# RG-LRU gate products as four 64x64 quadrants instead of block-diagonal 128x128 weights

## The chip, the cores and the metric

The kernel runs on one core of a Trainium2 chip. The metric is the time of one execution on the device in microseconds (us). Three runs of the kernel before are given, with their median.

## What is computed

The reference is a trunk of two layers of width 1024 on 512 latent and 256 context tokens (768 tokens in all). Each layer normalizes and modulates its input, projects it into three groups of heads (latent attention, a bidirectional mLSTM, a bidirectional RG-LRU), joins their outputs in one projection, and ends with an MLP. The change is in the RG-LRU. Its 256 channels form four blocks of 64, and each gate multiplies each block by its own 64x64 weights:

```python
LRU_BLOCKS, LRU_BD = 4, 64
...
def gates(xs, d):
    r = jax.nn.sigmoid(block_diag(xs, w_a[d], b_a[d]))
    i = jax.nn.sigmoid(block_diag(xs, w_x[d], b_x[d]))
```

`xs` is the branch's input after a convolution over four tokens; `d` is one of two directions. From `r` come the decay of a linear recurrence over the tokens (a = exp(-8 r softplus(-lam))) and the factor sqrt(1 - a^2); the recurrence runs over a and sqrt(1 - a^2) times i times xs, once forward and once backward, and the two results are added.

## The kernel before, in words

Channels lie on the 128 partitions and tokens on the columns, context first. The program is written as parts (Python generators) that yield an estimate of the time of what they have just emitted. `weave` takes a step of whichever part is behind, so parts are emitted side by side; a tile framework then sets the order on each engine and the semaphores. Engines are PE (TensorE), DVE (VectorE), ACT (ScalarE), POOL (GpSimd) and SP (SyncE, which issues most DMAs).

The stage of a layer that matters here (line 1172) weaves these parts:

- `in_kvq` makes keys and values of the mLSTM: products `kvp` (L178) of 128 tokens by 256 channels, in three passes over split weights (`whi`, `wlo`) and split inputs (`uh`, `ul`). For each of two halves there are six blocks of tokens with 24 matmuls each. ACT copies the results out (`kt` at L503, `vt` at L505). The weights are loaded by SP (L155), cast by ACT (`whi`, L158), and DVE takes the difference (`wlo`, L159).
- `ml_gates` (from L656) computes the mLSTM's gates. POOL's DMAs fetch `ig` and `fg` (L667); ACT takes three functions (L670 to L672); DVE makes `lf` (L674) and scans over `m` (L682, L684) and `bb` (L687, L688), then `st` and `bb` (L695, L697), the sum `lf` (L705); ACT takes exponentials into `st` (L706 for the first table `st1`, L717 for the second, `st2`, whose argument `ig` DVE makes in L710 to L716). PE transposes both tables into `colp` (L726), DVE copies that out (`colt`, L728), and PE makes `woldp` (L741).
- `lru` (L563) is the RG-LRU.
- In layer 0 only, a filler `mod_vec` makes modulation vectors: SP loads `modw` (512 KB a step, L247), PE multiplies (`modp`, L249, four matmuls on four groups of 32 columns); at the end of a vector DVE copies `modst` (L254) and PE transposes it (`modt`, L257).

In `lru` the convolution of a chunk of 128 channels (two blocks of 64) runs on DVE (L596, L599) into `xs`. For each direction and each gate (r, then i) PE makes one psum tile `lrup` (L608): a matmul on the 256 context columns and one on the 512 latent columns, whose 128x128 weights hold two 64x64 blocks on the diagonal and zeros elsewhere. There are 2 layers x 2 chunks x 2 directions x 2 gates = 16 such products. ACT turns each into `sig` with a Tanh (L613). Then ACT takes an exponential `lru_a` (L622) and a Tanh (L623), DVE multiplies (L624, L628, L629), ACT takes square roots (L633, L635), DVE multiplies (L640) and scans (L642, L645), and L649 adds the two directions.

The tiles `lru_a` and `lru_w` share a pool of three buffers (tag `aw`); the `lrup` tiles and the others of two banks share three psum buffers (tag `p2`). The weights `lruw` of a layer are one DMA of 512 KB (L565).

Of the kernel before, what the change touches and what calls it, by code (L numbers as in the profile page):

```python
# [9 lines left out]
F32 = mybir.dt.float32  # L10
F32R = mybir.dt.float32r
I32 = mybir.dt.int32
AF = mybir.ActivationFunctionType
# [4 lines left out]
L = 2  # L18
# [9 lines left out]
# how fast parts of the program go beside others, by layer  # L28
# [32 lines left out]
def trunk_kernel(ctx, tc, ins, out, dbg=None):  # L61
# [42 lines left out]
    # x^T, chunks of 128 channels, tokens [context | latent]  # L104
# [9 lines left out]
    # adds up rows r, 32 + r, 64 + r, 96 + r  # L114
# [6 lines left out]
    # ------------------------------------------------------------------ interleaving  # L121
    # A part of the program is a generator that yields about how long (us) what it emitted takes.
# [16 lines left out]
    def weave(*gens):  # L139
        """emit parts side by side, at equal pace; a filler only as long as the others last."""  # L140
# [10 lines left out]
    # ---------------------------------------------------------- small helpers  # L151
    def split_raw(src, shape):
        """(hi, lo) of weights from DRAM: hi has the bits that one pass of a product carries."""
# [8 lines left out]
    def split_act(src, a, b, tag, name, shape=None, tag2=None, after=None):  # L162
        """(hi, lo) of src, into columns a:b of new tiles: hi by ScalarE, lo by VectorE."""
# [11 lines left out]
    def mm3(dst, w, r, first, last):  # L175
        """dst += w.T @ r from the (hi, lo) parts of both."""
        for i, (a, b) in enumerate(PASSES):
            mm(dst, w[a], r[b], start=first and i == 0, stop=last and i == 2)  # L178

    def dense(ps, wk, rk, segs, M=128, po=PO):  # L180
        """ps[:M, po + t] = sum_k wk[k].T @ rk[k][:, t]; wk, rk: lists of (hi, lo)."""
# [8 lines left out]
    def rsqrt(v, n):  # L190
        """v ** -0.5 for n columns."""
# [4 lines left out]
    class Norm:  # L196
        """(mean of squares over channels + eps) ** -0.5 of each token, on every partition."""
# [17 lines left out]
        def columns(self, seg, out=None):  # L215
            """by tokens on partitions, a column per block of 128."""
# [9 lines left out]
        def spread(self, seg, ps, y):  # L226
            """on every partition, tokens along the columns."""
# [7 lines left out]
    # ------------------------------------------------------------- modulation  # L235
# [6 lines left out]
    def mod_vec(l, v, pace):  # L242
        """one of the six modulation vectors of a layer, a step per 128 rows of its weights."""
# [24 lines left out]
    def mod_rows(rows):  # L268
        """silu of both conditions along the columns, on every partition."""
# [10 lines left out]
    def mod_dot(l, v, pace, rows):  # L280
        """one of the six modulation vectors of a layer, a step per 128 of its channels."""
# [18 lines left out]
    def mod_load(j, tags):  # L300
        """the weights of 256 channels of the first two modulation vectors of the first layer."""
# [994 lines left out]
```

## Time and profile before

| | us |
|---|---|
| runs of the kernel | 1642.92, 1652.01, 1648.88 |
| median | 1648.88 |
| span of the profiled execution, from its first to its last recorded instruction | 1647.5 |
| PE busy in it | 1600.6 (97%) |
| DVE busy | 1075.7 (65%) |
| ACT busy | 583.2 (35%) |
| POOL busy | 63.6 (4%) |

The page gives no other time of the profiled execution than its span, so the span stands for it here; the median of the runs is 1.4 us above it. The trace gives each instruction's start and duration, grouped where the same instruction follows itself, and for idle time the engine and line that ended it. Several records belong to one matmul where its operands are f32 (a matmul of the gate products leaves two).

### The profile page before, as it was taken

The page shows a single profiled execution, that of the slowest core. Times are in us where ns is not written, and L with a number is a line of the kernel's source. Part 1 is how long each engine was busy: PE and PEld are TensorE (multiplying, and loading weights), DVE is VectorE, ACT ScalarE, POOL GpSimd, SP SyncE. Part 2 cuts the span into 40 slices and gives each one's busy share as a digit, 9 for nine tenths or more (in the row PEclk, how much of TensorE's full clock was granted, in tenths as well). Part 3 has the DMA queues.
Part 4 walks back from the last instruction along what each step waited for, and adds up shares of the span by engine and source line. Part 5 has one row for each costly group of instructions (what it writes and reads, how often), then busy time and mean ns, then how long its engine had stood idle before and what let it go on. Part 6 is the DMA issues. An engine that isn't in the chain of part 4 may idle for free.

```text
span 1647.5 us, 23128 instructions
## 1 busy us (share of the span) xinstructions
PE 1600.6 (97%) x9202; PEld 1335.2 (81%) x9202; DVE 1075.7 (65%) x2122; ACT 583.2 (35%) x878; POOL 63.6 (4%) x106
## 2 busy tenths in 40 slices
PE   8998999999999999999999998999999999999997
PEld 4666897788788888888888886887788888888887
DVE  4784577766797676666666478966877644444446
ACT  4462224444442212222122146622645432323223
POOL 1201010000000000000000001101000000000000
PEclk9999999999999999999999999999999999999998
DMA  9447111101344343333333131322102323222222
GB/s 314 129 158 231 64 58 47 50 14 63 105 146 149 116 141 115 109 122 118 134 120 128 65 116 40 89 70 77 65 14 90 116 90 102 90 94 99 90 103 102
DMA packets 58587, 170.48 MB, mean 103 GB/s; under 512 B 6720, under 2 KB 19776, under 8 KB 58480
## 3 DMA queue, kind: packets, MB, share of 16 engines
q1 hardware_dynamic: 55216, 161.26, 28.6%
q0 software_dynamic: 2112, 6.70, 1.4%
q8 instruction: 72, 1.18, 0.3%
q10 hardware_dynamic: 1152, 1.05, 0.2%
q14 instruction: 35, 0.29, 0.1%
HBM read 165.44 MB, written 2.15 MB: 102 GB/s over the span
## 4 chain that ended last, share of the span: by engine, by line
PE 81%; issue 2%; DVE 2%; ACT 1%; DMA 1%; POOL 0%; POOLq 0%; DVEq 0%; ACTq 0%
PE ff L186 51%; PE inp L186 6%; PE outp L186 6%; PE first L440 3%; PE py L178 2%; PE S L998 2%; PE kvp L178 2%; PE pT L1020 1%; PE S L1002 1%; PE pn L841 1%; PE S L1000 1%; PE qrp L186 1%; DMA modjunk<-in_crow 1%; PE sT L818 1%; PE lrup L608 1%
## 5 line engine op out<-in xcount | busy, mean ns | idle before, releaser
L158 ACT CAST whi<-raw 128x1024 fp32r<-128x1024 f32 x191 | 200.6, 1051 | 721.6 <-PE ff L186 578.6
L159 DVE TENSOR_TENSOR wlo<-raw,whi 128x1024 fp32r<-128x1024 f32 x191 | 233.1, 1221 | 158.4 <-ACT whi L158 153.9
L186 PE MATMUL ff<-hh,whi 128*128 128x512 f32 (+1 forms) x800 | 242.2, 348 | 0.0
L186 PE MATMUL ff<-hl,whi 128*128 128x512 f32 (+1 forms) x800 | 242.0, 348 | 0.0
L186 PE MATMUL ff<-hh,wlo 128*128 128x512 f32 (+1 forms) x800 | 242.0, 348 | 0.0
L289 DVE SCALAR_TENSOR_TENSOR modjunk<-modw,cb 128x512 f32<-128x512 f32 x224 | 154.7, 690 | 106.3 <-DMA modw<-in_w_modT 101.3
L186 PE MATMUL ff<-uh,whi 128*128 128x512 f32 (+1 forms) x696 | 210.9, 357 | 1.0 <-ACT hrelu L1077 1.0
L186 PE MATMUL ff<-uh,wlo 128*128 128x512 f32 (+1 forms) x696 | 210.2, 356 | 0.0
L186 PE MATMUL ff<-ul,whi 128*128 128x512 f32 (+1 forms) x696 | 209.4, 355 | 0.0
L408 DVE SCALAR_TENSOR_TENSOR x<-ff,mod,x 128x256 f32<-128x256 f32 (+1 forms) x200 | 123.1, 639 | 103.1 <-PE ff L186 103.0
L186 PEld LDWEIGHTS ff<-hl,whi 128*128 128x128 f32 x800 | 150.4, 188 | 20.8
L186 PEld LDWEIGHTS ff<-hh,wlo 128*128 128x128 f32 x800 | 150.3, 188 | 20.6
L186 PEld LDWEIGHTS ff<-hh,whi 128*128 128x128 f32 x800 | 150.3, 188 | 20.5
L186 PEld LDWEIGHTS ff<-uh,whi 128*128 128x128 f32 x696 | 130.8, 188 | 21.8 <-ACT hrelu L1077 1.7
L186 PEld LDWEIGHTS ff<-uh,wlo 128*128 128x128 f32 x696 | 131.0, 188 | 20.6 <-DVE wlo L159 0.5
L186 PEld LDWEIGHTS ff<-ul,whi 128*128 128x128 f32 x696 | 130.7, 188 | 20.5
L186 PE MATMUL inp<-uh,whi 128*128 128x256 f32 (+1 forms) x224 | 71.6, 376 | 3.7 <-ACT whi L158 3.7
L186 PE MATMUL inp<-ul,whi 128*128 128x256 f32 (+1 forms) x224 | 69.1, 366 | 0.0
L186 PE MATMUL inp<-uh,wlo 128*128 128x256 f32 (+1 forms) x224 | 68.8, 364 | 0.3 <-DVE wlo L159 0.3
L193 POOL TENSOR_TENSOR rsq<-rsv,nhalf 128x2 f32<-128x2 f32 (+2 forms) x16 | 14.2, 886 | 1310.1 <-DVE rsv L223 1308.6
L178 PE MATMUL kvp<-whi,uh 128*128 128x256 f32 x192 | 60.0, 313 | 4.2 <-ACT sig L613 2.9
L440 PE MATMUL first<-uh,wlo 128*128 128x256 f32 (+3 forms) x192 | 61.9, 325 | 0.6 <-DVE wlo L159 0.6
(316 smaller groups left out, 2767.2 us busy)
## 6 DMA issues: line engine op xcount, KB each, us to landing
raw<-in_w_ff2c SPq DMA_DIRECT2D x72, 512.0 KB, 3.5
raw<-in_w_ff1c SPq DMA_DIRECT2D x64, 512.0 KB, 3.5
modw<-in_w_modT SPq DMA_DIRECT2D x56, 512.0 KB, 3.7
modw<-in_w_mod SPq DMA_DIRECT2D x24, 512.0 KB, 4.4
raw<-in_w_outc SPq DMA_DIRECT2D x24, 512.0 KB, 3.5
raw<-in_w_inc SPq DMA_DIRECT2D x21, 512.0 KB, 3.5
modw<-in_w_mod SPq DMA_DIRECT2D x32, 256.0 KB, 5.1
raw<-in_w_inkv SPq DMA_DIRECT2D x8, 512.0 KB, 3.5
```

What stands on the lines that cost most here:

```text
L158: nc.scalar.copy(hi, raw)
L159: V.tensor_tensor(lo, raw, hi.bitcast(F32), op=OP.subtract)
L178: mm(dst, w[a], r[b], start=first and i == 0, stop=last and i == 2)
L186: mm(ps[:M, po + t0:po + t1], wk[k][a], rk[k][b][:, t0:t1], start=(k == 0 and i == 0), stop=(k == n - 1 and i == 2))
L289: V.scalar_tensor_tensor(junk, w[:, 512 * i:512 * i + 512], 1.0, rows[2 * r + i], op0=OP.mult, op1=OP.mult, accum_out=acc[:, m, i, r:r + 1])
L408: V.scalar_tensor_tensor(x[m][:, s[0]:s[1]], ps[:, po + s[0]:po + s[1]], modv[l][:, v, m, r:r + 1], x[m][:, s[0]:s[1]], op0=OP.mult, op1=O ...
L440: mm(ps[:M, PO + s[0]:PO + s[1]], wk[k][a][:, :M], self.rk[k][b][:, s[0]:s[1]], start=(k == 0 and i == 0), stop=(k == NK - 1 and i == 2))
L608: mm(ps[:, PO + a:PO + b], wl[:, g, d, c], xs[:, a:b], start=True, stop=True)
L818: mm(sT[h][:, PO + 128 * b:PO + 128 * b + 128], kT[p][hp, bs], z["q"][p][hp, bs], start=True, stop=True)
L841: mm(w["pn"][:, 65 * b:65 * b + 65], wT[:, 128 * b:128 * b + 128], z["vt"][p][:, b, j], start=True, stop=True)
L998: mm(S[:, PO + a:PO + e], z["qk"][h][wa][:, qs], ckv[ra][:, a:e], start=(i == 0), stop=False)
L1000: mm(S[:, PO + a:PO + e], z["qr"][h][:, qs], kr[0][:, a:e], start=False, stop=False)
```

## The change

The block-diagonal weights go. TensorE's array is used as four quadrants of 64x64: the upper or lower half of the partitions feeds it, the left or right half of the columns comes out. The weights `lruw` hold gate r's blocks on partitions 0 to 63 and gate i's on 64 to 127, half of the bytes of before (256 KB a layer). Row half g therefore always computes gate g, and it needs both blocks of channels on its own 64 partitions. Block o on partitions 64 o is there in `xs` for g = o; for the other two quadrants two DMAs on POOL's queue copy `xs` into a tile `xsw` with its halves exchanged (64 partitions x 768 x 4 bytes = 192 KB each). `xsw` takes one of the three `aw` buffers. Per direction both gates' psum tiles are made together by eight matmuls of 64x64, and two Tanh follow. The steps yield 0.65 instead of 1.3, so the weaving of the other parts around them moves too.

```diff
@@ def lru(l, z, t0):
-        wl = wp.tile([128, 2, 2, 2, 128], F32, tag="raw", bufs=3, name="lruw")
+        wl = wp.tile([128, 2, 2, 128], F32, tag="raw", bufs=3, name="lruw")
...
+            sw = slot("aw", "xsw")
+            for g in range(2):
+                gdma(sw[64 * g:64 * g + 64], xs[64 - 64 * g:128 - 64 * g])
             sg, sp_ = {}, {}
             for d in range(2):
+                pss = [ps2("lrup") for _ in range(2)]
+                for a, b in BOTH:
+                    for g in range(2):
+                        for o in range(2):
+                            rows, outs = slice(64 * g, 64 * g + 64), slice(64 * o, 64 * o + 64)
+                            mm(pss[g][outs, PO + a:PO + b], wl[rows, d, c, outs], (xs if g == o else sw)[rows, a:b],
+                               start=True, stop=True)
                 for g in range(2):
-                    ps = ps2("lrup")
-                    for a, b in BOTH:
-                        mm(ps[:, PO + a:PO + b], wl[:, g, d, c], xs[:, a:b], start=True, stop=True)
                     st = slot("ls", "sig", shape=[SB // 4])
...
-                    act(s, ps[:, PO:], AF.Tanh, scale=0.5, bias=hb[:, 4 * g + 2 * d + c:4 * g + 2 * d + c + 1])
+                    act(s, pss[g][:, PO:], AF.Tanh, scale=0.5, bias=hb[:, 4 * g + 2 * d + c:4 * g + 2 * d + c + 1])
                     sg[d, g] = s
-                    yield 1.3
+                    yield 0.65
...
@@ layout of the weights on the host
-    wl = np.zeros((L, 128, 2, 2, 2, 128), f)
+    wl = np.zeros((L, 128, 2, 2, 128), f)
...
-                wl[:, o:o + 64, gi, d, b // 2, o:o + 64] = i[nm][:, d, b]
+                wl[:, 64 * gi:64 * gi + 64, d, b // 2, o:o + 64] = i[nm][:, d, b]
```

Dependencies in the changed program: the copies wait for the last step of the chunk's convolution on DVE; the second chunk's `xsw` takes the buffer of the first chunk's `lru_w`, so it waits for DVE's product `sig<-sig,lru_w` (L640 of before); the psum tiles of the second direction wait for the Tanh of the first.

The order on the engines changes in the two stages with keys and values alone. On PE in layer 0, where the first chunk's gates are made, before:

```order
L608 MATMUL lrup_705<-xs_672,lruw_630 128x256
L178 MATMUL kvp_712<-whi_604,uh_168 128x256
L178 MATMUL kvp_712<-wlo_605,uh_168 128x256
L178 MATMUL kvp_712<-whi_604,ul_169 128x256
L178 MATMUL kvp_712<-whi_604,uh_170 128x256
L178 MATMUL kvp_712<-wlo_605,uh_170 128x256
L178 MATMUL kvp_712<-whi_604,ul_171 128x256
L608 MATMUL lrup_719<-xs_672,lruw_630 128x256
L249 MATMUL modp_663<-modw_692,cs_92 32x256 x4
L608 MATMUL lrup_705<-xs_672,lruw_630 128x512
L608 MATMUL lrup_719<-xs_672,lruw_630 128x512
```

And with the change:

```order
L615 MATMUL lrup_708<-xs_672,lruw_630 64x256
L249 MATMUL modp_663<-modw_692,cs_92 32x256 x4
L249 MATMUL modp_663<-modw_751,cs_92 32x256 x4
L615 MATMUL lrup_708<-xsw_705,lruw_630 64x256
L615 MATMUL lrup_708<-xs_672,lruw_630 64x512
L615 MATMUL lrup_708<-xsw_705,lruw_630 64x512
L249 MATMUL modp_663<-modw_787,cs_92 32x256
L615 MATMUL lrup_709<-xsw_705,lruw_630 64x256
L615 MATMUL lrup_709<-xs_672,lruw_630 64x256
L615 MATMUL lrup_709<-xsw_705,lruw_630 64x512
L615 MATMUL lrup_709<-xs_672,lruw_630 64x512
```

The key/value products that stood between the gate matmuls now come behind all eight of the first direction; only products for the modulation stand among them.

On DVE in layer 1, from the chain of the mLSTM's gates to the sum `lf` (`sig` and `gb` belong to the RG-LRU), before:

```order
L599 SCALAR_TENSOR_TENSOR xs_9100<-xp_8502,cols_74,xs_9100 128x256
L682 SCALAR_TENSOR_TENSOR m_8860<-lf_8765,ig_8766 4x768
L684 SCALAR_TENSOR_TENSOR m_8860<-lf_8765,ig_8766 4x256
L687 SCALAR_TENSOR_TENSOR bb_8862<-fg_8768,lf_8765 4x768
L684 SCALAR_TENSOR_TENSOR m_8860<-lf_8765,m_8860,ig_8766 4x512
L688 SCALAR_TENSOR_TENSOR bb_8862<-fg_8768,lf_8765 4x768
L624 SCALAR_TENSOR_TENSOR sig_8876<-sig_8876,xs_8821 128x768
L695 TENSOR_TENSOR st1_8920<-ig_8766,bb_8862 36x768
L628 TENSOR_TENSOR gb_8819<-lru_a_8933 128x768
L697 TENSOR_TENSOR bb_8862<-bb_8862,m_8860 36x768
L629 SCALAR_TENSOR_TENSOR gb_8819<-gb_8819,sig_8857 128x768
L705 TENSOR_TENSOR lf_8765<-st1_8920,bb_8862 4x768 x2
```

And with the change, where the next row is the sum `lf` (L714 there):

```order
L159 TENSOR_TENSOR wlo_9126<-raw_9123,whi_9125 128x1024
L691 SCALAR_TENSOR_TENSOR m_8892<-lf_8787,ig_8788 4x768
L693 SCALAR_TENSOR_TENSOR m_8892<-lf_8787,ig_8788 4x256
L633 SCALAR_TENSOR_TENSOR sig_8905<-sig_8905,xs_8843 128x768
L693 SCALAR_TENSOR_TENSOR m_8892<-lf_8787,m_8892,ig_8788 4x512
L696 SCALAR_TENSOR_TENSOR bb_8894<-fg_8790,lf_8787 4x768
L697 SCALAR_TENSOR_TENSOR bb_8894<-fg_8790,lf_8787 4x768
L637 TENSOR_TENSOR gb_8841<-lru_a_8939 128x768
L704 TENSOR_TENSOR st1_8959<-ig_8788,bb_8894 36x768
L638 SCALAR_TENSOR_TENSOR gb_8841<-gb_8841,sig_8889 128x768
L706 TENSOR_TENSOR bb_8894<-bb_8894,m_8892 36x768
L633 SCALAR_TENSOR_TENSOR sig_8928<-sig_8928,xs_8843 128x768
```

A difference of weights (`wlo`) has come in ahead of the scans, and a second product `sig` ahead of `lf`; the piece of the convolution has gone ahead of the rows shown.

On ACT in layer 1, from the exponential of `st1` on, before:

```order
L706 ACTIVATE st1_8920<-lf_8765 36x768
L717 ACTIVATE st2_8921<-ig_8766 36x768
L503 COPY kt_8740<-kvp_8982 128x128
L503 COPY kt_8741<-kvp_8982 128x128
L158 CAST whi_9088<-raw_9086 128x1024
L633 ACT_TABLE_LOAD
L633 ACTIVATE lru_w_9000<-lru_w_9000 128x768
L635 ACTIVATE gb_8819<-gb_8819 128x768
```

And with the change:

```order
L715 ACTIVATE st1_8959<-lf_8787 36x768
L503 COPY kt_8762<-kvp_9020 128x128
L503 COPY kt_8763<-kvp_9020 128x128
L642 ACT_TABLE_LOAD
L642 ACTIVATE lru_w_8988<-lru_w_8988 128x768
L726 ACT_TABLE_LOAD
L726 ACTIVATE st2_8960<-ig_8788 36x768
L644 ACT_TABLE_LOAD
L644 ACTIVATE gb_8841<-gb_8841 128x768
```

The square root of `lru_w` now stands between the two exponentials, with a table load ahead of it and one behind it.

## Rows read from the trace of the kernel before

**Rows 1.** The page: busy time of each engine, its share of the span, instructions.

```profile
PE 1600.6 (97%) x9202; PEld 1335.2 (81%) x9202; DVE 1075.7 (65%) x2122; ACT 583.2 (35%) x878; POOL 63.6 (4%) x106
```

**Rows 2.** Chain of waits, layer 1: start us, us, what.

```profile
1022.03 2.56 PE lrup L608 x4
...
1025.92 1.29 PE lrup L608 x4
1027.21 5.19 PE kvp L178 x44
1032.40 1.65 issue
```

**Rows 3.** Timeline of PE, layer 0: start, us, instruction, [idle before, releaser].

```profile
102.31 0.44 PE L257 MATMUL modt<-ident,modst 128*128 128x128 f32 x2 [3.93 <-DVE modst L254]
...
113.47 0.39 PE L178 MATMUL kvp<-whi,uh 128*128 128x256 f32 x1
...
140.28 0.88 PE L186 MATMUL inp<-uh,whi 128*128 128x256 f32 x2 [2.24 <-ACT whi L158]
```

**Rows 4.** Timeline of PE, layer 1.

```profile
1020.57 0.39 PE L178 MATMUL kvp<-whi,uh 128*128 128x256 f32 x1 [2.90 <-ACT sig L613]
...
1034.05 0.70 PE L726 MATMUL colp<-ident,st 100*128 100x100 f32 x6 [1.65 <-issue]
...
1036.13 0.71 PE L726 MATMUL colp<-ident,st 100*128 100x100 f32 x6 [0.17 <-issue]
```

**Rows 5.** Timeline of PE, layer 0, ahead of the first gate product.

```profile
71.67 0.28 PE L178 MATMUL kvp<-wlo,uh 128*128 128x256 f32 x1
71.88 0.64 PE L249 MATMUL modp<-modw,cs 128*32 128x256 f32 x8
...
72.67 0.28 PE L178 MATMUL kvp<-whi,uh 128*128 128x256 f32 x1
```

**Rows 6.** DMA issues from 66 to 100 us: transfer, count, KB, us to landing.

```profile
fg<-kg POOLq DMA_DIRECT2D x2, 12.0 KB, 3.2
```

**Rows 7.** DMA issues from 1060 to 1080 us.

```profile
sig<-kg POOLq DMA_DIRECT2D x2, 192.0 KB, 4.3
```

**Rows 8.** DMA issues from 120 to 140 us.

```profile
sig<-kg POOLq DMA_DIRECT2D x2, 192.0 KB, 10.0
```

**Rows 9.** Stretches: length, busy PE, PEld, DVE, ACT, POOL, granted clock, DMA share, GB/s.

```profile
73.00:80.00 7.00, 6.77 (x46) 4.27 (x45) 5.92 (x11) 6.68 (x9) 1.27 (x4) 1.00 0.73 198
...
130.00:140.00 10.00, 6.64 (x57) 5.07 (x56) 5.19 (x23) 2.95 (x5) 0.06 (x1) 1.00 0.96 286
...
1020.00:1025.00 5.00, 4.43 (x16) 3.22 (x17) 4.91 (x4) 3.96 (x7) 0.28 (x3) 0.66 0.01 3
```

**Rows 10.** Timeline of DVE, layer 0.

```profile
73.24 0.75 DVE L599 SCALAR_TENSOR_TENSOR xs<-xp,cols,xs 128x512 f32<-128x512 f32 x1
...
81.30 1.75 DVE L687 TENSOR_TENSOR_SCAN bb<-fg,lf 4x768 f32<-4x768 f32 x1
82.98 0.92 DVE L624 SCALAR_TENSOR_TENSOR sig<-sig,xs 128x768 f32<-128x768 f32 x1
...
93.89 0.94 DVE L640 SCALAR_TENSOR_TENSOR sig<-sig,lru_w 128x768 f32<-128x768 f32 x1
```

**Rows 11.** Timeline of DVE, layer 1.

```profile
1012.75 1.22 DVE L159 TENSOR_TENSOR wlo<-raw,whi 128x1024 fp32r<-128x1024 f32 x1
...
1019.22 0.47 DVE L599 SCALAR_TENSOR_TENSOR xs<-xp,cols,xs 128x256 f32<-128x256 f32 x1
...
1031.18 1.90 DVE L705 TENSOR_TENSOR lf<-st,bb 4x768 f32<-4x768 f32 x2
```

**Rows 12.** Timeline of ACT, layer 1.

```profile
1018.33 1.28 ACT L613 ACT_TABLE_LOAD   x1
1019.62 1.69 ACT L613 ACTIVATE sig<-lrup,lrub 128x768 f32<-128x768 f32 x2
...
1035.18 0.85 ACT L717 ACTIVATE st<-ig 36x768 f32<-36x768 f32 x1 [1.23 <-DVE ig L716]
```

## The prediction

> **What bounds the kernel now.** I read the shares of busy time first: TensorE (PE) is busy 97% of the span [rows 1], so a change counts if it alters what PE has to do or what PE waits for. The gate products run only in the two stages that also make keys and values, so I then read the chain of waits through the stage of layer 1 [rows 2]. A product of 128x128 weights on 768 columns is two matmuls and takes 1.29 us; 44 key/value products of 256 columns take 5.19, that is 0.118 each. Sixteen gate products are 16 x 1.29 = 20.6 us of 1647.5, and they are all that the change can save on PE. But the same chain shows 1.65 us in which PE waits before the transposes of the gate columns. PE's own timeline [rows 3, 4] shows more such waits: 3.93 in layer 0 (for DVE's copy modst) and 2.90 in layer 1 (for ACT's sigmoid). Together that is 8.5 us. In these stages PE is one of three partners: conv and recurrence on DVE, sigmoids on ACT, products on PE.
>
> **The products themselves.** Before: per direction and gate a matmul of 256 and one of 512 columns, 0.43 + 0.86 = 1.29. Now: per direction eight matmuls of 64x64, two psum tiles. No row shows four quadrants beside each other. The bounds: one after another, 8 x 1.29 / 2 = 5.16 per direction and chunk, 41.2 in all, a loss of 20.6; all four together 1.29 per direction and chunk, 10.3, a gain of 10.3. I take quadrants to overlap, because the nearest row has it: the eight records of modp (four matmuls of 256 columns on four column groups of 32) end in 0.64 us [rows 5], where one after another they would take 4 x 0.43 = 1.7. In the order as emitted the four do not always line up (the rows of PE's order): where a piece waits for the copy, or 256 stands beside 512 in the same quadrant, a group takes 1.72 rather than 1.29, and the first one, split by modp, 3.0. Adding up the eight groups gives 15.0: a gain of 5.6.
>
> Changing between quadrants and full products also has a price. Around one modp, key/value products start at 71.67 and 72.67 [rows 5]; with 2 x 0.118 for the two products between, 0.77 is left for modp, of which 0.43 is streaming by the width of its columns. So an excursion costs 0.34 beside its streaming. Some ten excursions to the quadrants cost 3.4 (ends: 0, if modp's own loading of weights is in it, and 6.8, if each takes it twice). Net on PE: -5.6 + 3.4 = **-2.2**.
>
> By the Trainium skill, "TensorEngine Tiling (Array Packing)", Key Properties, a change of tiling mode drains TensorE, which speaks against short excursions; modp's row with 0.34 agrees, though it shows column groups only. Without that drain the products alone would give -5.6.
>
> **The copies.** Each chunk's xs is now copied with halves exchanged, two DMAs of 192 KB issued by POOL. POOL is 4% busy [rows 1], so issuing costs nothing by itself; what counts is when they land. Landing times of POOL's DMAs: 12 KB took 3.2 in the same stage, 192 KB 4.3 in layer 1 and 10.0 in layer 0 [rows 6 to 8], the last where the DMA engines are 0.96 busy; the stretch in question has 0.73 [rows 9]. So between 3.2 and 10.0 I take 5.0 for layer 0's first chunk, nearest to the 4.3, and 4.0 to 4.5 elsewhere.
>
> By the Trainium skill, "DMA: Bandwidth & Descriptors", section on the SWDGE path, such a transfer costs about 2.0 us plus its bytes over 436 GB/s, which for 192 KB is an estimate of 2.4. The rows of this trace are longer (4.3 and 10.0). By the page's figure the first place below would be some 2 us less, and the end about 1654.
>
> **Layer 0, first chunk.** The conv on DVE ends at 73.24 + 0.75 = 74.0 [rows 10]. The copies leave then and land at 79.1. The quadrant groups of direction 1 run with a modp piece between (1.29 + 0.77 + 1.29): PE is through at 82.4, ACT's second sigmoid (0.85) at 83.3. DVE's next instruction is the product of this gate with xs, and behind it now stand the mLSTM scans. Before, DVE went through from 82.98 to the end of the row at 93.89, 11.8 us; in the new order the stretch also holds the scan of 1.75 over m, its piece of 0.7 and the second scan over bb (1.75), which before came ahead of it, and lacks two rows of 0.9 and 0.7. That is 14.4: 83.3 + 14.4 = 97.7.
>
> **Layer 0, second chunk.** Its copies need a buffer that the row of 97.7 frees, so they land at about 102 and PE does direction 1 until 103.3. That wait hides behind another: modt needs modst from DVE, before at 102.31 [rows 3], 7.5 after the row at 93.89 had ended. Now two more DVE instructions (0.9 each) stand ahead: 97.7 + 7.5 + 1.8 = 107.0. From modt to the kvp at 113.47 PE took 11.2, of which seven of eight gate matmuls are 4.7; now 1.7 for one group: 107.0 + 11.2 - 4.7 + 1.7 = 115.2. The second half's weights wait for ACT's cast, which stands behind the last sigmoid and the exponentials (by my walk of its queue until 115.1), and for DVE's difference of 1.22 [rows 11]: 116.4. Before, 138 key/value products were left at 113.47; now 143 at 116.4. Lag 2.9 + 5 x 0.118 = **+3.5**. PE then waits in the stretch of full DMA engines (2.24 [rows 3], for weights); the stream of those weights restarts as much later, so I let nothing be absorbed.
>
> **Layer 1.** The first chunk's copies land by 1017.5 and its products end about 1019; ACT, which is loading a table until then, cannot take the first sigmoid before 1019.62 anyway [rows 12], so PE goes on at 1020.57 as before [rows 4]. What is late is the chain of gate columns. On DVE (the rows of its order) a weights' difference (1.22) and the second sigmoid product (0.92 in [rows 10]) now come ahead of the sum lf, and a conv piece of 0.47 [rows 11] goes: +1.7. The first colp moves from 1034.05 to 1035.7. On ACT (the rows of its order) two table loads (1.28 each [rows 12]) and a square root (0.85, taken like the exponential's row) now stand between the exponentials of st1 and st2. Lf ends at 1031.18 + 1.90 + 1.7 = 1034.8; exponential 0.85, load 1.28, root 0.85, load 1.28, exponential 0.85 end at 1039.9, with the two key copies between at about 1040.2. The second colp, before at 1036.13, comes then: **+4.1**, and PE has no other work queued that could run ahead of it. The second chunk's copies land behind that wait; its products cost 4 x 1.29 before and 1.29 + 1.72 + 2 x 0.34 now: -1.5. After so long a wait I add +1.2 for one group at half clock: the group at 1022.03, after 2.90 of idle time, took 2.56 instead of 1.29, which is the lower of the two levels (1.2 instead of 2.4 GHz), with a granted clock of 0.66 in that stretch [rows 2, 9]. Layer 1: +4.1 - 1.5 + 1.2 = **+3.8**. Until the next such wait PE runs nearly without idle time, so the lag stays.
>
> **Sum.** +3.5 + 3.8 = +7.3. The profiled execution spans 1647.5; the median of the three runs (1648.9) is 1.4 above it. 1647.5 + 7.3 + 1.4 = **1656**.
>
> **Rivals.**
> - *Row halves in turn.* Two column halves overlap, row halves do not: a group takes 2.58, no product is saved. Against it nothing but the design; for it, no row shows two row halves together. Added where products stand on the path: three times 0.86 and 1.29 and 0.86, +4.7: 1661. Chance 0.20.
> - *Layer 0's lag is absorbed* where PE waits for the DMA engines (2.24 and the like): the weights come no later than before. It decides if their loads are issued as before. -3.5: 1652.5. Chance 0.15.
> - *The waits only change their names, and PE's net gain counts:* the wait for modst and that for colp grow by no more than the products shrink, so the end moves by -2.2, to 1646.7. It decides where the idle time of PE in the two stages stays at 8.5 or below. For it: ACT could load its tables while it waits for DVE. Against: the loads stand between two exponentials that wait for one another. Chance 0.12.
> - *The quadrants run one after another:* the change doesn't do what it says, +26: 1682. Chance 0.03.
>
> **How the numbers follow.** The forecast has 0.50. What a measurement of this kernel can tell from no change is about 0.5%, 8.2 us: below 1640.6 is faster, above 1657.1 slower. The forecast itself is 0.8 below that bound and goes beyond it if copies take 6 or more, so 0.4 of its chance is slower; with 0.9 of the first rival, 0.1 of the second and all of the last: 0.20 + 0.18 + 0.02 + 0.03, 0.43. Faster needs more than the third rival gives: 0.06, if excursions cost nothing and the waits stay. The range takes in the third rival at the lower end and the first, with a copy of 10 us at one place, at the upper: 1645 to 1665.
>
> **What would show it.** Right: 64x64 records that start in pairs or fours; an idle row on PE of some us for xsw in layer 0's first chunk and none in layer 1; modt near 107; the second colp four us after the first. Wrong: landing of xsw above 6 or below 3; pieces of one group that follow each other; modp and kvp that start without gap after quadrants; colp at its old place.

## The result and the profile after

| | us |
|---|---|
| changed kernel, four runs | 1664.41, 1662.63, 1659.96, 1659.35; median 1661.3 |
| kernel before, four runs | median 1648.7 (1642.92 to 1652.01) |
| ratio | 1.0081, 95% interval 1.0056 to 1.0106 |
| span of the profiled execution | 1662.6 (its own time 1664.41, the longest of the four) |

The change costs 0.81%, about 13 us; the forecast was 1656, some 5 us too low. Of all executions below one, of e2, ran with a mean granted clock of 0.563 and took 2565.18 us; the ratios leave it out. Busy time on the page of the changed kernel, against [rows 1]:

```profile
PE 1608.6 (97%) x9266; PEld 1334.3 (80%) x9266; DVE 1075.6 (65%) x2122; ACT 586.9 (35%) x881; POOL 68.4 (4%) x113
```

The share says nothing: PE's is as high as before. To place the loss, three marks in PE's timeline are needed: the first key/value product (kvp) of layer 0, the first of layer 1, and the end.

| | start to kvp of layer 0 | layer 0's part | layer 1's part |
|---|---|---|---|
| before | 67.17 | 939.89 | 640.44 |
| after | 71.28 | 946.85 | 644.47 |
| difference | +4.1 | +7.0 | +4.0 |

The first column is not the change's: up to that mark the program is the same, and the same program took 64.9 to 67.1 in the other kernels' profiles below. So after's times in layer 0 are compared with before's 4.1 later, and in layer 1 11.1 later. Parts of a single execution carry some us of their own: a kernel with the changed kernel's layer 0 (e4) showed 943.7 instead of 946.9.

The stretches of the two parts (columns as in [rows 9]: length, busy time of PE first, granted clock third from the end), before and after:

```profile
67.17:1007.06 939.89, 921.37 (x5568) 784.27 (x5568) 647.70 (x1348) 305.25 (x447) 27.29 (x44) 0.99 0.31 107
1007.06:1647.50 640.44, 620.43 (x3354) 516.24 (x3354) 394.17 (x693) 250.68 (x387) 23.89 (x38) 0.99 0.25 85
```

```profile
71.28:1018.13 946.85, 927.25 (x5601) 783.53 (x5601) 646.78 (x1348) 305.66 (x447) 29.95 (x48) 0.98 0.33 106
1018.13:1662.60 644.47, 619.89 (x3386) 515.72 (x3386) 395.00 (x693) 253.96 (x390) 26.01 (x41) 0.98 0.27 86
```

In layer 0 PE's idle time (length less busy time) grew by 1.1 us only, its busy time by 5.9, although the gate products need less: there the loss is mostly slower running. In layer 1 idle time grew by 4.6 and busy time fell by 0.5.

Timeline of PE after, layer 0:

```profile
78.92 0.64 PE L249 MATMUL modp<-modw,cs 128*32 128x256 f32 x8 [1.04 <-DMA modw<-in_w_mod]
81.86 1.08 PE L249 MATMUL modp<-modw,cs 128*32 128x256 f32 x8 [2.30 <-DMA modw<-in_w_mod]
83.22 0.69 PE L615 MATMUL lrup<-xsw,lruw 64*64 64x256 f32 x1 [0.28 <-DMA xsw<-xs]
...
89.72 0.58 PE L178 MATMUL kvp<-whi,uh 128*128 128x256 f32 x1
...
111.49 0.49 PE L615 MATMUL lrup<-xsw,lruw 64*64 64x256 f32 x1 [3.37 <-DMA xsw<-xs]
...
117.05 0.44 PE L257 MATMUL modt<-ident,modst 128*128 128x128 f32 x2
...
171.52 0.38 PE L257 MATMUL modt<-ident,modst 128*128 128x128 f32 x2
```

The copies land at 83.2, in before's time 79.1. Ahead of their readers PE has stood 1.04 and 2.30 for weights of the modulation, since two steps `modp` come first in its queue and no key/value products. The second step ended at 82.94, before the copies landed, so by themselves these waits delayed nothing. The stretches show what followed:

```profile
77.00:83.00 6.00, 2.60 (x21) 0.64 (x19) 5.41 (x11) 5.51 (x7) 1.52 (x3) 0.83 0.87 255
83.00:90.00 7.00, 6.78 (x17) 1.97 (x18) 0.34 (x2) 1.06 (x2) 3.19 (x6) 0.50 0.38 116
90.00:95.00 5.00, 5.00 (x27) 2.82 (x28) 4.23 (x4) 3.48 (x4) 0.00 (x0) 0.53 0.00 0
```

PE was busy 2.60 of 6.00 us, and in the twelve after that the granted clock is 0.50 to 0.53, the lower of the two levels: of the first chunk's gate products all but the first matmul (64x256, at 77.23) run at 1.2 GHz. DVE, busy 0.34 of 7.00 us, waits for them (its timeline):

```profile
90.77 0.96 DVE L633 SCALAR_TENSOR_TENSOR sig<-sig,xs 128x768 f32<-128x768 f32 x1 [7.25 <-ACT sig L622]
...
104.48 0.94 DVE L649 SCALAR_TENSOR_TENSOR sig<-sig,lru_w 128x768 f32<-128x768 f32 x1
```

From there to the row that frees the second copy's buffer takes 14.65. Landing times after (DMA issues from 66 to 120 us, and in the second fence, for layer 1's first chunk, from 1010 to 1035 us):

```profile
xsw<-xs POOLq DMA_DIRECT2D x4, 192.0 KB, 5.4
```

```profile
xsw<-xs POOLq DMA_DIRECT2D x2, 192.0 KB, 3.1
```

In layer 0 the first chunk's pair took 5.1 and the second's 5.5; in layer 1 it was 3.1 and 3.6.

Timeline of PE after, layer 1, against [rows 4], and a group of the second chunk at the full clock:

```profile
1027.37 0.43 PE L615 MATMUL lrup<-xsw,lruw 64*64 64x256 f32 x1 [1.64 <-DMA xsw<-xs]
...
1046.85 1.19 PE L735 MATMUL colp<-ident,st 100*128 100x100 f32 x6 [2.76 <-ACT st L715]
1051.67 1.23 PE L735 MATMUL colp<-ident,st 100*128 100x100 f32 x6 [3.63 <-issue]
...
1062.68 0.59 PE L615 MATMUL lrup<-xs,lruw 64*64 64x512 f32 x1
1062.87 0.43 PE L615 MATMUL lrup<-xsw,lruw 64*64 64x256 f32 x1
1062.88 0.43 PE L615 MATMUL lrup<-xs,lruw 64*64 64x256 f32 x1
1062.88 0.64 PE L615 MATMUL lrup<-xsw,lruw 64*64 64x512 f32 x1
```

The second colp comes 4.8 after the first, where before it was 2.1. The last four rows are four quadrants beside each other. ACT between the exponentials, against [rows 12] (its timeline):

```profile
1045.95 0.84 ACT L715 ACTIVATE st<-lf 36x768 f32<-36x768 f32 x1 [4.23 <-DVE lf L714]
...
1047.27 1.28 ACT L642 ACT_TABLE_LOAD   x1
1048.57 0.84 ACT L642 ACTIVATE lru_w<-lru_w 128x768 f32<-128x768 f32 x1
1049.43 1.28 ACT L726 ACT_TABLE_LOAD   x1
1050.72 0.84 ACT L726 ACTIVATE st<-ig 36x768 f32<-36x768 f32 x1
```

With both colp late, PE falls to the lower clock here too. The stretch behind the first colp after, and in the second fence one of the kernel before, behind its stage:

```profile
1047.00:1057.00 10.00, 6.37 (x43) 5.83 (x43) 9.85 (x17) 6.89 (x9) 1.07 (x2) 0.50 0.16 41
```

```profile
1118.00:1124.00 6.00, 5.84 (x24) 4.25 (x25) 5.11 (x22) 0.63 (x1) 1.04 (x1) 0.72 0.19 72
```

The last key/value product of layer 1 starts at 1079.78, before at 1062.62: the stage ends 6.1 late. Of that 1.5 comes back where the kernel before ran at 0.72 (1118 to 1124) and the changed kernel, at the same work (1133 to 1140), at 1.00, another 0.5 at the very end; the part ends 4.0 late.

### The profile page after: what moved, and what is told of

It is laid out like the page before. It is cut to its first block, busy times and chain, and to the rows that moved or that the text cites. A ratio compares the mean times of both kernels' runs of the same rounds, so it can differ in the third digit from the quotient of the medians.

```text
span 1662.6 us, 23284 instructions
## 1 busy us (share of the span) xinstructions
PE 1608.6 (97%) x9266; PEld 1334.3 (80%) x9266; DVE 1075.6 (65%) x2122; ACT 586.9 (35%) x881; POOL 68.4 (4%) x113
## 4 chain that ended last, share of the span: by engine, by line
PE 79%; DVE 3%; issue 3%; ACT 2%; DMA 1%; POOL 0%; POOLq 0%; DVEq 0%; ACTq 0%
PE ff L186 51%; PE inp L186 6%; PE outp L186 6%; PE first L440 3%; PE py L178 2%; PE S L1007 2%; PE pT L1029 1%; PE kvp L178 1%; PE S L1011 1%; PE pn L850 1%; PE S L1009 1%; DVE wlo L159 1%; PE qrp L186 1%; PE sT L827 1%; PE pi L838 1%
## 5 line engine op out<-in xcount | busy, mean ns | idle before, releaser
L440 PE MATMUL first<-uh,whi 128*128 128x256 f32 (+3 forms) x192 | 61.5, 331 | 1.2 <-ACT n2sq L212 0.6
```

The costliest lines, as they stand in the source:

```text
L440: mm(ps[:M, PO + s[0]:PO + s[1]], wk[k][a][:, :M], self.rk[k][b][:, s[0]:s[1]], start=(k == 0 and i == 0), stop=(k == NK - 1 and i == 2))
```

## The experiments

Twelve kernels, in four groups (e1 to e4, e5 to e8, e9 and e10, e11 and e12); with each group the kernel before ran on the same chip (medians 1645.8, 1648.2, 1647.4, 1646.9). "Parts" are layer 0's and layer 1's as above, from one profiled execution each.

| kernel | median | ratio, 95% interval | layer 0 | layer 1 |
|---|---|---|---|---|
| before | | 1 | 939.9 | 640.4 |
| the change | 1661.3 | 1.0081 (1.0056 to 1.0106) | 946.9 | 644.5 |
| e1 no copies | 1649.9 | 1.0016 (1.0003 to 1.0030) | 934.8 | 645.1 |
| e2 full products, new structure | 1652.4 | 1.0039 (1.0026 to 1.0051) | 932.5 | 648.1 |
| e3 own buffer | 1656.9 | 1.0050 (1.0032 to 1.0068) | 944.2 | 644.6 |
| e4 square root behind | 1661.2 | 1.0093 (1.0071 to 1.0115) | 943.7 | 646.1 |
| e5 steps 1.3 | 1657.9 | 1.0060 (1.0033 to 1.0086) | 943.5 | 648.7 |
| e6 steps 1.3, own buffer | 1650.2 | 1.0018 (0.9998 to 1.0038) | 939.7 | 642.8 |
| e7 gates first, own buffer | 1659.7 | 1.0064 (1.0039 to 1.0090) | 946.6 | 646.2 |
| e8 kernel before, steps 0.65 | 1654.0 | 1.0025 (1.0010 to 1.0041) | 939.6 | 645.9 |
| e9 as e6, room for the copy | 1651.8 | 1.0027 (1.0012 to 1.0042) | 940.3 | 645.9 |
| e10 as e1, steps 1.3 | 1645.1 | 0.9984 (0.9968 to 0.9999) | 937.0 | 638.6 |
| e11 as e6, copy by POOL | 1650.7 | 1.0024 (1.0010 to 1.0039) | 941.1 | 642.3 |
| e12 as e6, copy by DVE | 1649.1 | 1.0017 (1.0001 to 1.0032) | 935.7 | 644.0 |

**e1: no copies.**

```diff
-            sw = slot("aw", "xsw")
-            for g in range(2):
-                gdma(sw[64 * g:64 * g + 64], xs[64 - 64 * g:128 - 64 * g])
...
-                            mm(pss[g][outs, PO + a:PO + b], wl[rows, d, c, outs], (xs if g == o else sw)[rows, a:b],
+                            mm(pss[g][outs, PO + a:PO + b], wl[rows, d, c, outs], xs[rows, a:b],
```

> Leaves out the exchange of halves: all four quadrants read xs itself, so two of the four blocks multiply the wrong channels; the copies and their buffer are gone, the 64x64 matmuls and their number stay. Measured by two parts of the span that leave the start of the kernel out: from the first kvp of layer 0 to the first kvp of layer 1 (939.9 us before, 946.9 with the change) and from there to the end (640.4 and 644.5). If the copies' waits and the half clock behind them make layer 0's loss (my theory), the first part falls to 939 to 942; the second stays at 643 to 645, since the square root still stands between the two exponentials: 1652 to 1655 in all. If the quadrant products and the changes of mode make the loss (rival), the first part stays at 945 or above and the time near 1661.

Layer 0's part fell to 934.8 and the time to 1649.9, both even below what I expected, and the ratio from 1.0081 to 1.0016; layer 1's part stayed at 645.1. So layer 0's loss comes with the copies, and layer 1's does not. The rival falls.

**e2: block-diagonal 128x128 weights in the changed structure.**

```diff
-        wl = wp.tile([128, 2, 2, 128], F32, tag="raw", bufs=3, name="lruw")
+        wl = wp.tile([128, 2, 2, 2, 128], F32, tag="raw", bufs=3, name="lruw")
...
                 pss = [ps2("lrup") for _ in range(2)]
-                for a, b in BOTH:
-                    for g in range(2):
-                        for o in range(2):
...
+                for g in range(2):
+                    for a, b in BOTH:
+                        mm(pss[g][:, PO + a:PO + b], wl[:, g, d, c], xs[:, a:b], start=True, stop=True)
```

> Keeps the change's structure (both gates' psum tiles of a direction made together, steps of 0.65) but with the block-diagonal 128x128 weights and no copies. If the new order alone costs the time (rival), it stays at 1658 or above. If the copies and quadrants do in layer 0 (my theory), the first part is 939 to 942; the second part, where the table loads stand between the exponentials here too, stays at 643 to 645: 1652 to 1655. If only the quadrants cost, it is back at 1649.

The time is as expected, the split by parts is not: layer 1 lost 7.7 us without a quadrant or a copy in it. Its two colp stand 4.81 apart (1028.31 and 1033.12), as in the changed kernel. Layer 0's part came out lower than I can account for (932.5); its one execution was 2 us under the kernel's median.

**e3: own buffer for the copy.**

```diff
-            sw = slot("aw", "xsw")
+            sw = slot("z", "xsw")
```

> Takes the copy's tile from another pool (tag z), so that the second chunk's copy no longer waits for the buffer of lru_w. My theory: the wait of 3.37 us on PE for xsw in layer 0 goes, but modst is late by DVE's queue, which waits 7.25 for the first chunk's sigmoids; so the first part gains 0 to 2: 945 to 947. Rival, that the buffer is the tight place: the first part falls by 3.4 or more, to 943.5 or less.

The wait of 3.37 is gone; the first wait after the first chunk is now for modst (3.12). Layer 0's part is 944.2, between the two expectations; by the ratios the buffer is worth about 0.3% (1.0081 against 1.0050, with overlapping intervals), more than I gave it.

**e4: layer 1's square roots held back behind st2.**

```diff
+            yield from until(lambda: l == 0 or "st2" in z)
+            with tc.issue_after(z["st2"].ins) if l else nullcontext():
-            late = act(wv[1], wv[1], AF.Sqrt, scale=-1.0)
+                late = act(wv[1], wv[1], AF.Sqrt, scale=-1.0)
...
-        act(st2[0:R], w2, AF.Exp)
+        z["st2"] = act(st2[0:R], w2, AF.Exp)
```

> In layer 1 alone the first chunk's square roots are held back behind the exponential of st2, so no table load stands between the two exponentials; layer 0 is as with the change. My theory (the two loads and the root make the second colp late): the second colp follows the first by about 2.0 to 2.5 us instead of 4.8, and the second part falls from 644.5 to 641.5 to 642.5. Rival (the chain on DVE that makes the argument of st2 is the limit, and the two interleaved products on DVE): it falls by less than 1.

My theory fails here. Timelines of PE and, in the second fence, of DVE:

```profile
1039.01 0.74 PE L738 MATMUL colp<-ident,st 100*128 100x100 f32 x6 [4.29 <-ACT st L718]
1042.93 1.23 PE L738 MATMUL colp<-ident,st 100*128 100x100 f32 x6 [3.17 <-issue]
```

```profile
1038.12 0.96 DVE L638 TENSOR_TENSOR lru_w<-lru_a 128x768 f32<-128x768 f32 x1
...
1039.18 0.96 DVE L639 SCALAR_TENSOR_TENSOR lru_w<-lru_w,sig 128x768 f32<-128x768 f32 x1
...
1041.41 0.54 DVE L728 TENSOR_TENSOR ig<-bb,m 4x384 f32<-4x384 f32 x1
```

With the table loads out of the way the second colp is still 3.92 behind the first: the argument of st2 is ready only at 1041.95, because DVE has two RG-LRU products (0.96 each) in that chain. The loads hid a limit on DVE that was 0.9 us shorter. Nor is the gap between the two colp the loss itself: in e3 the second follows by 1.49 (1041.47 and 1042.96), and layer 1's part is 644.6 as with the change. Holding the RG-LRU back costs it later; layer 1's part rose to 646.1.

**e5: steps back to 1.3**, and **e6** with the own buffer of e3 as well.

```diff
-                    yield 0.65
+                    yield 1.3
```

> The change with its steps of 0.65 put back to 1.3, nothing else; the quadrants, the copies and their buffer stay. In its order the roots of layer 1 stand behind the exponential of st2, and in layer 0 the products for the modulation still stand ahead of the quadrants that read the copy. If the shorter steps make layer 1's loss (my theory now), the second part (first kvp of layer 1 to the end) falls from 644.5 to 640 to 642, and layer 0's part stays at 943 to 947: about 1656 to 1659. If the copies or the quadrants make layer 1's loss (rival), the second part stays at 643.5 or above.

> Steps of 1.3 and the copy's tile in its own pool together. My theory: the two gains add, some 3 us in each layer: 1651 to 1654. Rival (the first chunk's wait in layer 0 decides, the buffer not): as with the steps alone, 1656 to 1659.

Alone, the steps give a quarter of the loss back (1.0060, with overlapping intervals): layer 1's part did not fall but rose to 648.7. In e5's timeline of PE the second chunk's copy has become the wait:

```profile
1037.59 0.71 PE L735 MATMUL colp<-ident,st 100*128 100x100 f32 x6 [3.03 <-issue]
1039.99 1.20 PE L735 MATMUL colp<-ident,st 100*128 100x100 f32 x6
...
1052.52 0.68 PE L615 MATMUL lrup<-xsw,lruw 64*64 64x256 f32 x1 [2.37 <-DMA xsw<-xs]
```

The colps are 2.4 apart, as the steps should make them, but the copy waits for the buffer of a chain that now comes later. With both edits (e6) the ratio is 1.0018, no difference that could be told, and a little less time than I expected. The fall of 0.63% is 0.1 more than the two gains added (0.31 in e3, 0.21 here), which lies within the uncertainty.

**e7: layer 1's gates paced ahead**, with the own buffer.

```diff
-PACE = {"gates": (1.0, 0.79), "lru": (0.67, 0.86), "mod": (1.76, 0.0), "ml": (1.21, 0.73),
+PACE = {"gates": (1.0, 0.6), "lru": (0.67, 0.86), "mod": (1.76, 0.0), "ml": (1.21, 0.73),
```

> Own pool for the copy, steps of 0.65, and in layer 1 the mLSTM's gates are paced ahead (factor 0.6 instead of 0.79), so that their chain on DVE comes ahead of the RG-LRU's products. My theory (the late transposes of the gate columns are layer 1's loss): the second part falls to 640 to 642 and the wait on PE ahead of the second colp to under 1.5: 1652 to 1655. Rival (something else in layer 1): 644 or above.

The waits ahead of both colp are gone, as expected. But the time is not won, and by its parts the rival holds. Timeline of PE:

```profile
1034.62 0.68 PE L615 MATMUL lrup<-xsw,lruw 64*64 64x256 f32 x1 [8.19 <-ACT sig L622]
1043.40 0.68 PE L735 MATMUL colp<-ident,st 100*128 100x100 f32 x6
...
1046.48 0.68 PE L735 MATMUL colp<-ident,st 100*128 100x100 f32 x6
```

PE now waits 8.19 us for the first direction's Tanh, whose psum tiles the second direction needs. The two chains share DVE and ACT; putting one ahead makes the other the wait.

**e8: the kernel before with steps of 0.65 and nothing else.**

```diff
-                    yield 1.3
+                    yield 0.65
```

> The kernel before with nothing but its step after each gate product cut from 1.3 to 0.65. ACT's order in layer 1 then has the square root with its table loads between the two exponentials, as with the change. If the order alone makes layer 1's loss (my theory), the second part rises from 640.4 to 643.5 to 648, layer 0's part stays, and the time is 0.2 to 0.45% above the kernel before. Rival (copies or quadrants are needed for it): no difference.

As expected in every number. Timeline of PE, to be held beside [rows 4]:

```profile
1034.99 0.73 PE L726 MATMUL colp<-ident,st 100*128 100x100 f32 x6 [2.40 <-ACT st L706]
1039.80 1.23 PE L726 MATMUL colp<-ident,st 100*128 100x100 f32 x6 [4.08 <-issue]
```

One estimate, with no instruction added or taken away, puts the colps 4.81 apart and costs layer 1 5.5 us, 0.25% in all. That layer 0's part stays hides something: its third modt comes 3.1 earlier after the layer's first kvp than before (89.6 against 92.7), and the layer gives that back behind the stage.

**e9: a step of 6.0 after the copies**, on top of e6.

```diff
                 gdma(sw[64 * g:64 * g + 64], xs[64 - 64 * g:128 - 64 * g])
+            yield 6.0
```

> Steps of 1.3, own pool for the copy, and a step of 6.0 after the two copies are issued, so that key and value products are emitted between the copies and the quadrants. In its order of PE in layer 0 fifteen key and value rows and one modulation step less stand between the first weights that are late and the quadrants. My theory (layer 0's loss is PE waiting for modulation weights and copies with nothing else to do, and then running at the lower clock): the waits of 0.6, 1.8 and 1.7 us before the first quadrants go to under 1 in all, the first part falls from 939.7 to 934 to 938, the second stays at 640 to 643: 1643 to 1648, within 0.3% of the kernel before. Rival (the quadrants themselves cost layer 0's time): the first part stays at 939 or above.

Layer 0's waits went as expected, and the clock stayed up. Timeline of PE and stretches:

```profile
71.49 0.64 PE L249 MATMUL modp<-modw,cs 128*32 128x256 f32 x8 [0.26 <-DMA modw<-in_w_mod]
...
76.82 0.64 PE L249 MATMUL modp<-modw,cs 128*32 128x256 f32 x8 [0.66 <-DMA modw<-in_w_mod]
...
97.45 0.44 PE L257 MATMUL modt<-ident,modst 128*128 128x128 f32 x2 [1.93 <-DVE modst L254]
...
145.22 0.64 PE L249 MATMUL modp<-modw,cs 128*32 128x256 f32 x8 [2.53 <-DMA modw<-in_w_mod]
...
158.73 0.63 PE L257 MATMUL modt<-ident,modst 128*128 128x128 f32 x2
```

```profile
72.00:80.00 8.00, 7.34 (x59) 4.93 (x55) 5.53 (x11) 5.86 (x10) 2.13 (x4) 1.00 0.89 266
80.00:90.00 10.00, 9.57 (x85) 5.99 (x85) 9.87 (x10) 7.75 (x11) 0.63 (x3) 1.00 0.49 140
```

In e6 the same stretch ran at the lower clock:

```profile
77.00:80.00 3.00, 2.68 (x6) 0.74 (x6) 2.97 (x4) 0.63 (x1) 2.46 (x6) 0.50 0.85 253
80.00:85.00 5.00, 5.00 (x16) 2.13 (x16) 2.23 (x3) 1.97 (x3) 0.84 (x2) 0.50 0.33 82
```

And yet layer 0's part is 940.3 against 939.7. The modulation tells where it went. The first modt comes 31.0 us after the layer's first kvp (66.44) in e9, 38.3 in e6, 35.1 before. The third comes 92.3, 92.8 and 92.7 after it; before, it is this row:

```profile
159.88 0.63 PE L257 MATMUL modt<-ident,modst 128*128 128x128 f32 x2
```

What e9 won by 97 it has given back by 159: between its second and its third modt PE waits 2.53 for the modulation's weights and 1.91 for those of the products `inp`, where e6 waits 0.45, and its granted clock is 0.72 from 144 to 150, in e6 1.00. My expectation for this part fails, and so does the explanation of layer 0's loss by the waits of the first chunk alone: with steps of 1.3 and an own buffer, what they cost is made up within the stage. That the stream of weights holds the third modt near 92.5 is not shown: in e10 it comes after 88.9, in e2 after 87.6. In the changed kernel the third modt comes 100.2 after (171.52 - 71.28), 7.5 later than before, and that is the 7.0 of the layer. In layer 1 the same step made the gates' chain late (PE waits 6.42 for the first colp).

**e10: no copies, steps of 1.3** (the edit of e1 and that of e5).

> Quadrants without the exchange of halves (all four read xs, two blocks multiply the wrong channels) and steps of 1.3: what the 64x64 products are worth when neither copies nor short steps stand in the way. My theory: PE's net gain shows, 2 to 5 us below the kernel before: 1643 to 1646, first part 933 to 936, second 639 to 641. Rival (changes of mode eat the gain): no difference from the kernel before.

0.16% below the kernel before, with 1 just outside the interval; layer 0's part is 1 us above what I expected, layer 1's a little below. The gate products alone, as groups of instructions over the whole kernel, before and in e10:

```profile
L608 PE MATMUL lrup<-xs,lruw 128*128 128x256 f32 (+1 forms) x64 | 25.5, 519 | 1.2 <-ACT kt L503 0.9 <-ACT sig L613 0.2
```

```profile
L612 PE MATMUL lrup<-xs,lruw 64*64 64x256 f32 (+1 forms) x128 | 18.8, 546 | 0.9 <-ACT sig L619 0.8
```

25.5 us of PE become 18.8. The time won is 2.6 (0.16% of 1647), so some of the 6.7 goes elsewhere. The changes of mode would have it so, but no run takes them apart from other waits.

**e11 and e12: the exchange by instructions instead of DMAs**, on top of e6.

```diff
-                gdma(sw[64 * g:64 * g + 64], xs[64 - 64 * g:128 - 64 * g])
+                nc.gpsimd.tensor_copy(sw[64 * g:64 * g + 64], xs[64 - 64 * g:128 - 64 * g])
```

(in e12 the same on DVE)

> The exchange of halves by two copies of 64 partitions x 768 on POOL itself instead of two DMAs; steps of 1.3 and own pool as in the run with both. If the landing time of the DMAs (4 to 5.4 us) is what is left of the loss (my theory), PE's waits for xsw fall to under 1 us a chunk, the first part to 936 to 938, the second to 639 to 641: 1644 to 1647, at or a little below the kernel before. Rival (POOL is slower at such a copy than the DMA, or DVE is held up beside it): waits for xsw stay at 1.5 us or more and the time at 1650.

> The same with the two copies on DVE. A copy of 64 partitions x 768 I put at 0.5 to 0.9 us by the rows of 128 x 768 (0.94), so DVE gets 4 to 7 us more work in all, some of it on the chain of the gate columns. My theory: no wait for xsw above 1 us, the second part 0.5 to 1.5 above that with POOL's copies: 1645 to 1649. Rival (DVE's queue is the limit of both stages): each copy shows in full, 1650 or above.

e11 at 1.0024 is what the rival said in the time, though not by its wait: xsw holds PE up 0.69 at most; PE's longest wait is 6.04 for DVE's modst in layer 0, where e10 has 3.87. Two copies on POOL, and two on DVE in e12 (timelines of POOL and DVE):

```profile
1012.30 2.63 POOL L606 COPY xsw<-xs 64x768 f32<-64x768 f32 x2 [3.15 <-DVE xs L600]
```

```profile
1012.61 1.14 DVE L606 COPY xsw<-xs 64x768 f32<-64x768 f32 x2
```

2.63 for a pair on POOL and 1.14 on DVE, where the DMA needs 2.8 to 3.6 in the same layer (in e6 and in the changed kernel). So POOL hardly shortens the copy, and e12 is the better test. e12 lies at 1.0017, at the upper edge of what I expected; its layer 0 is good (935.7). In layer 1 PE stands 2.83 for xsw at 1013.22, where I expected no wait above 1: the copies are short, but on DVE the convolution ahead of them ends only at 1012.60. Later DVE is late for the next weights as well (2.43 on PE for wlo at 1043.33). Neither beats the kernel before. What they leave over e10 (0.33 to 0.40%) is not the landing time of a DMA, since neither has one for the copy. They rest on other orders as well, so the cause of that remainder stays open.

**The loss in parts.** Along one path each edit's share is a difference of ratios: the quadrants alone -0.16% (e10); the copies +0.34% (e6 - e10); the short steps +0.32% (e3 - e6); the shared buffer +0.31% (change - e3). In us of 1648 that is -2.6, +5.6, +5.3 and +5.1, 13.4 together. Each difference is uncertain by some 0.2 to 0.3%, and by another path the shares move (the steps alone are +0.25% in e8; taken away first, in e5, they gave back 0.2%): the waits stand in for one another.

**The lower clock beside the waits.** Each profile also records when the granted clock stood at 0.50. In layer 0's part that was 30.7 us with the change and 17.1 before; in layer 1's, without the last 20 us, 13.7 and 6.8. Key/value products start 0.21 apart then (1054.16 to 1054.38) instead of 0.12, so half of what was added, 6.8 and 3.4 us, is an estimate of the most that this can have cost, against +7.0 and +4.0. In the table e2 has least of it in layer 0 (6.8) and the shortest part (932.5), e5 the most in layer 1 (27.3) and the longest (648.7). The stretches shown for the change stand behind waits of PE, and in e9, without the waits, the first chunk ran at 1.00; but no run holds the clock still, so how much of the loss is the clock's stays an estimate.

## Why the prediction was right or wrong

- **The time.** 1661.3 lies in the range of 1645 to 1665, above the 1657.1 from which the prediction calls the kernel slower (chance 0.43). The forecast itself, 1.004 times the kernel before, lies below the measured interval. The rival *row halves in turn* gives 1661 too, but that is chance: its mechanism falls (next item).
- **The products: right, as far as the interval tells.** Forecast -5.6, +3.4 for the changes of mode, net -2.2. Measured without copies and with the old steps: -2.6 (-0.2 to -5.3). The four quadrants run beside each other, both halves of the rows included, so the rivals "row halves in turn" and "one after another" fall. By the Trainium skill, "TensorEngine Tiling (Array Packing)", Key Properties, different tiles work in parallel; the rows at 1062.68 to 1062.88 agree.
- **The copies: right for the first chunk.** Forecast 5.0 and a landing at 79.1 (74.0 + 5.0 is 79.0); the trace has 5.1 and 79.1 (83.2 less the 4.1). Elsewhere I had 4.0 to 4.5; it was 5.5 in layer 0 and 3.1 and 3.6 in layer 1. By the Trainium skill, "DMA: Bandwidth & Descriptors", section on the SWDGE path, it would have been an estimate of 2.4; the runs show 2.8 (in layer 1 of e6) to 5.5.
- **Layer 0, first chunk: the step that failed.** I had PE through at 82.4: from the copies' landing a group, 0.77 for one modp and a group, 3.35 in all at the full clock. It was through at 89.7, in before's time 85.6, so the same work took 6.5, because it ran at the lower clock. I had charged half clock in layer 1 only and put it at nothing here. What I left out is how PE waits for the landing: two modp steps stand ahead of it in the queue, without key/value products, and waited 1.04 and 2.30 for weights. These waits ended before the landing and delayed nothing by themselves; but PE was busy for only 2.60 of 6.00 us, and the lower clock came behind that. DVE's first product came at 86.7 instead of 83.3. What follows from it was sized right (14.65 on DVE; forecast 14.4).
- **Layer 0, second chunk: wrong in which wait ends last.** I had the copy at about 102, hidden behind modst at 107.0. It landed at 107.4; PE stood 3.37 for it, and modt came at 112.9 with no wait of its own.
- **"I let nothing be absorbed": wrong.** At the 168th of 288 key/value products (116.24 before; 130.67 after, less the 4.1) the changed kernel is 10.3 late; the layer ends 7.0 late. In e9 a lead of 7 us over e6 at the first modt is gone at the third. So +3.5 was +7.0 (3.8 by e4's layer 0), the sum of a lag three times as long and an absorption I had left out.
- **Layer 1: the number right in part by luck, the reason half right.** First colp forecast 1035.7, measured 1035.8; second 1040.2 and 1040.6; the layer +3.8 and +4.0. But from the second colp on I had -1.5 for the second chunk and +1.2 for half clock, a stage 3.8 late. It ended 6.1 late, with 10 us at the lower clock (0.50 from 1047 to 1057), and 1.5 came back where the kernel before ran at 0.72 and the changed one did not. I had also seen no wait for xsw in layer 1; PE stood 1.64 for it at 1027.37. e4 shows that DVE's chain was nearly as long as the table loads. And e8 shows that the shorter step is enough for such a loss, which the prediction told only by its effects on the order.
- **The rival on the other side** (waits only change their names, 1646.7) is what e6 comes near to with the two edits, and e10 is without the copies.
- **Sum.** 1656 against 1661.3: by the profiles layer 0 is mis-sized by up to 3.5: a lag of 10.3 instead of 3.5, of which the half clock made 3.2 in the first direction's products alone, less what was absorbed. The parts of the two profiled executions differ by 11.0, the medians by 12.6; the rest is within what the runs scatter. The bound of 1657.1 lies 1.1 above the forecast, not 0.8.

## What to carry to other kernels

Where estimates set the order of a schedule, halving a step with the work it stands for is itself a change: run the old kernel with the new estimate first (e8 cost 0.25% with no instruction changed). A copy ahead of its reader costs its landing time only if the queue holds nothing else: look at what stands between in the reader's queue, and whether that has to wait too. A gap in TensorE's work can cost more than its length: here the 12 us behind it ran at the lower clock. And a buffer borrowed from a pool ties the copy to whoever had it last; take that wait and the order together, since either alone may give nothing.

## What was not expected of the hardware

- A copy with exchanged halves needs no DMA: DVE moves 64 partitions x 768 from one half of the partitions to the other in 0.57 us (1.14 for two), POOL two in 1.90 to 3.54, against 2.8 to 5.5 for the DMA.
- After six us in which it was busy for 2.60, TensorE ran some 12 us at the lower clock although it was busy nearly all of that time (0.50 in 83 to 90, 0.53 in 90 to 95), where the work was mostly quadrants; in e9, without the waits, the same products ran at 1.00.
- The time to the first key/value product, for one and the same program, was 64.9 to 67.2 in thirteen profiles and 71.3 in one.
